# A decoder layer on one core: the split weights of each load at one of nine places in their buffers

## The chip, the core and the metric

The kernel runs on one core of a Trainium2 chip. The metric is the device time of one execution in microseconds (us). The profile is one execution of the program, recorded by the hardware profiler.

## The reference

One layer of a decoder (512 tokens, width 1024, float32): a SwiGLU feed-forward at half weight, a mixing block of three parallel head groups, a second SwiGLU feed-forward.

```python
def swiglu(x, w_gate, w_up, w_down):
    return (jax.nn.silu(x @ w_gate) * (x @ w_up)) @ w_down
...
x = x + 0.5 * swiglu(rms_norm(x, g_ffn1[l]), w_ffn1_gate[l], w_ffn1_up[l], w_ffn1_down[l])
h = rms_norm(x, g_mix[l])
proj = h @ w_in[l]
...
x = x + jnp.concatenate([y_attn, y_conv, y_mem], axis=-1) @ w_out[l]
x = x + 0.5 * swiglu(rms_norm(x, g_ffn2[l]), w_ffn2_gate[l], w_ffn2_up[l], w_ffn2_down[l])
```

The three groups are windowed attention with sinks, a causal depthwise convolution with LayerNorm, and cross-attention into 256 memory tokens. The feed-forward's inner width is 2816, that is 22 blocks of 128.

## The kernel before

Everything is kept transposed: channels on the 128 partitions, the 512 tokens along the free dimension. A float32 product is taken in three matmuls of type float32r. Each operand is split into a high half (rounded to float32r) and a low half (the rest), and `mm3` (line 339) and `product` (line 439) issue, for every block of 128x128 weights, high weights by high activations, high weights by low activations, low weights by high activations. Each of the three loads its weights anew. So TensorE's lists are long trains of triples: one weight load of 128 columns and one stream of 256 or 512 columns each.

The class `Weights` (line 86) brings the weights in. A load is 128 partitions by 1024 float32, by DMA from the SP queue into one of four raw buffers (`wraw`), up to three ahead. `split_to` (line 145) then splits it: ScalarE copies raw to the high half `hi` (line 167), VectorE writes raw minus hi to the low half `lo` (line 168). There are four pairs of buffers for halves, `whi0` to `whi3` and `wlo0` to `wlo3`, taken in turn (`self.turn`). Each has 1024 + 32 columns, so the 1024 that are used can begin anywhere in the first 128 bytes: `hi` begins at `off` bytes, `lo` at 128 - `off`. The caller gives `off` for each load: 0 for the gate and up weights of the first four blocks, the projections, the output weights and the memory values; 128 for the gate and up pairs that go through the sums, the down weights and the memory keys. A last kind of half load, `off=None`, goes to buffers of its own, `vhi` and `vlo`.

Where the buffers lie is read from the built program. Every `whi` buffer starts at a multiple of 256 bytes, every `wlo` buffer at 128 modulo 256. So with `off` 0 both halves begin at 0 modulo 256, with `off` 128 both begin at 128 modulo 256; the blocks within them follow at steps of 512 bytes. `vhi` and `vlo` lie at 128 modulo 256. The moving operands (`xh`, `xl`, `hh`, `hl`, `yh`, `yl`, `bh`, `bl`, `mh`, `ml`) all begin at 64 modulo 256.

The stages: in each feed-forward, blocks 0 to 3 are direct products of 512 columns (`xh`, `xl`). Blocks 4 to 21 go through `fast` (line 448), a scheme with seven products of half size, each of 256 columns with operands `bh` and `bl`, of which one takes `vhi` and `vlo`. The down products (`hh`, `hl`) come in six rounds, a part of the inner width each; those of the first round stream 512 columns, later ones 256 in two cuts. Between the two feed-forwards lies the mixing block, with 512-column products (`xh`, `xl`, then `yh`, `yl`) and the attention, the convolution and the norms in an order written out by hand. The memory keys and values (operands `mh`, `ml`, 256 columns) come at block 17 of the first feed-forward; for the values the weights are the moving operand and the memory the stationary one (lines 646 to 648).

The order on each engine is the order of the program text; a wait comes from buffers and data alone.

Of the kernel before, what the change touches and what calls it, by code (L numbers as in the profile page):

```python
# [85 lines left out]
class Weights:  # L86
# [58 lines left out]
    def split_to(self, n):  # L145
        nc = self.nc
        while self.done < min(n, len(self.items)):
            i = self.done
            need, cols, off, src = self.items[i]
            self.load_to(need + 1)  # L150
            if need in self.after:
                self.after.pop(need)()
            if off is None:
                hi, lo = (self.extra.tile([P, cols], F32R, tag=t, name=f"{t}{i}", bufs=1) for t in ("vhi", "vlo"))
            else:

                j = self.turn % self.bufs[1]
                self.turn += 1
                hi, lo = (
                    self.pool.tile([P, 1024 + 32], F32R, tag=f"{t}{j}", name=f"{t}{i}", bufs=1)[:, c : c + 1024]  # L160
                    for t, c in (("whi", off // 4), ("wlo", 32 - off // 4))
                )
            if i < self.by_hand:
                self.piece[i] = (src(), hi, lo)
            else:
                raw = src()
                nc.scalar.copy(hi[:, :cols], raw[:, :cols])  # L167
                nc.vector.tensor_tensor(lo[:, :cols], raw[:, :cols], hi[:, :cols].bitcast(F32), op=ALU.subtract)  # L168
            self.split[i] = (hi, lo)
            self.done += 1  # L170
            if i >= self.by_hand:
                self.load_to(need + 1 + self.dma_ahead)
# [1062 lines left out]
```

## Time and profile before

| | |
|---|---|
| time, two runs | 863.86 and 866.05 us, median 864.95 us |
| span of the profiled execution | 862.3 us |
| TensorE busy, weight loads busy | 855.5 us, 789.7 us |
| VectorE busy, ScalarE busy | 697.0 us, 446.1 us |
| TensorE clock granted | 1.00 |
| mean DMA rate | 106 GB/s |

The times are those of whole executions; the profiled execution is given by its span, the time from the first to the last instruction, which is 2.65 us below the median of the runs. PE stands for matmuls, PEld for weight loads, which overlap matmuls. Matmuls are pipelined, so the duration of one overlaps its neighbours. In groups, a row has the line, the engine, the operation, output and inputs by the program's names, shapes, count, busy time in us and mean in ns, and idle time before. In the timeline, a row has the start in us, the duration in us, engine, line, operation and names.

### The profile page before, as it was taken

What the parts mean: (1) busy time and instruction counts of PE and PEld (TensorE: products, weight loads), DVE (VectorE), ACT (ScalarE), POOL (GpSimd) and SP (SyncE); (2) the same over time, 40 slices, a digit from 0 to 9 for tenths busy, and PEclk for the clock granted to TensorE, in tenths of its full rate; (3) what the DMA queues carried; (4) which work ended last, traced back from release to release, by engine and by line L of the source; (5) the groups of instructions that cost most, each with busy time, mean ns of one, the idle gap of its engine ahead of it and who ended that gap; (6) DMA issues with size and microseconds to landing.
All of it is one profiled execution on the core that took longest, in us unless ns stands there. A gap on an engine that the chain in (4) does not pass through costs nothing.

```text
span 862.3 us, 15722 instructions
## 1 busy us (share of the span) xinstructions
PE 855.5 (99%) x6361; PEld 789.7 (92%) x6361; DVE 697.0 (81%) x1163; ACT 446.1 (52%) x741; POOL 27.4 (3%) x30
## 2 busy tenths in 40 slices
PE   9999999999999999999999999999999999999998
PEld 5889999999999999988776888889999999999998
DVE  7998877877868897869989985997887868787772
ACT  7455555455654444533948763454654544544540
POOL 0000000000000000300000030010000000000000
PEclk9999999999999999999999999999999999999999
DMA  7326333334553334222010423335333343323312
GB/s 273 123 78 168 97 100 122 100 112 133 142 143 120 123 110 130 74 98 62 5 57 14 133 75 103 94 91 154 99 98 123 98 122 97 109 92 100 120 49 99
DMA packets 34809, 91.45 MB, mean 106 GB/s; under 512 B 3248, under 2 KB 5808, under 8 KB 34736
## 3 DMA queue, kind: packets, MB, share of 16 engines
q1 hardware_dynamic: 32000, 85.99, 32.1%
q0 software_dynamic: 1584, 2.88, 2.1%
q10 hardware_dynamic: 1152, 1.57, 0.6%
q8 instruction: 50, 0.82, 0.4%
q14 instruction: 23, 0.19, 0.1%
HBM read 85.45 MB, written 2.10 MB: 102 GB/s over the span
## 4 chain that ended last, share of the span: by engine, by line
PE 92%; DVE 3%; ACT 2%; issue 1%; DMA 1%; SPq 0%; ACTq 0%; DVEq 0%
PE mm L347 14%; PE mm L349 14%; PE mm L348 14%; PE mm L444 11%; PE mm L445 11%; PE mm L446 11%; PE sc L444 2%; PE sc L445 2%; PE sc L446 2%; PE sc L349 1%; PE sc L347 1%; PE sc L348 1%; PE tp L948 1%; PE tp L962 1%; ACT p L913 1%
## 5 line engine op out<-in xcount | busy, mean ns | idle before, releaser
L444 PE MATMUL mm<-bh,whi 128*128 128x256 f32 x864 | 238.8, 276 | 0.2 <-ACT kept L459 0.2
L445 PE MATMUL mm<-bl,whi 128*128 128x256 f32 x864 | 238.5, 276 | 0.0
L446 PE MATMUL mm<-bh,wlo 128*128 128x256 f32 x864 | 238.5, 276 | 0.0
L348 PE MATMUL mm<-hl,whi 128*128 128x256 f32 (+1 forms) x640 | 183.9, 288 | 0.0
L349 PE MATMUL mm<-hh,wlo 128*128 128x256 f32 (+1 forms) x640 | 183.9, 288 | 0.0
L347 PE MATMUL mm<-hh,whi 128*128 128x256 f32 (+1 forms) x640 | 183.3, 288 | 0.0
L167 ACT CAST whi<-wraw 128x1024 fp32r<-128x1024 f32 (+2 forms) x122 | 124.2, 1021 | 102.5 <-PE mm L348 37.9
L168 DVE TENSOR_TENSOR wlo<-wraw,whi 128x1024 fp32r<-128x1024 f32 (+2 forms) x122 | 144.5, 1187 | 27.9 <-ACT whi L167 27.3
L444 PEld LDWEIGHTS mm<-bh,whi 128*128 128x128 f32 x864 | 162.2, 188 | 0.6 <-ACT kept L459 0.4
L445 PEld LDWEIGHTS mm<-bl,whi 128*128 128x128 f32 x864 | 162.2, 188 | 0.2
L446 PEld LDWEIGHTS mm<-bh,wlo 128*128 128x128 f32 x864 | 162.2, 188 | 0.0
L349 PEld LDWEIGHTS mm<-hh,wlo 128*128 128x128 f32 x640 | 120.2, 188 | 2.9
L347 PEld LDWEIGHTS mm<-hh,whi 128*128 128x128 f32 x640 | 120.2, 188 | 2.7
L348 PEld LDWEIGHTS mm<-hl,whi 128*128 128x128 f32 x640 | 120.2, 188 | 2.7
L168 DVE TENSOR_TENSOR wlo<-s,whi 128x1024 fp32r<-128x1024 f32 x72 | 87.9, 1222 | 34.7 <-ACT whi L167 34.4
L167 ACT CAST whi<-s 128x1024 fp32r<-128x1024 f32 x72 | 75.5, 1051 | 46.1 <-PE mm L445 42.3
L347 PE MATMUL mm<-xh,whi 128*128 128x512 f32 x192 | 76.6, 403 | 0.3 <-ACT whi L179 0.3
L348 PE MATMUL mm<-xl,whi 128*128 128x512 f32 x192 | 75.6, 394 | 0.6 <-DVE xl L359 0.5
L349 PE MATMUL mm<-xh,wlo 128*128 128x512 f32 x192 | 75.9, 395 | 0.0
L506 DVE SCALAR_TENSOR_TENSOR x<-mm,x 128x512 f32<-128x512 f32 x80 | 54.0, 682 | 3.3 <-PE mm L349 3.3
L167 ACT CAST vhi<-wraw 128x512 fp32r<-128x512 f32 x36 | 22.4, 622 | 60.9 <-PE sc L445 46.8
L126 DVE TENSOR_TENSOR s<-wraw 128x512 f32<-128x512 f32 x36 | 24.9, 691 | 33.5 <-DMA wraw<-in_wgu 33.5
(244 smaller groups left out, 1368.2 us busy)
## 6 DMA issues: line engine op xcount, KB each, us to landing
wraw<-in_wgu SPq DMA_DIRECT2D x86, 512.0 KB, 3.6
wraw<-in_wd SPq DMA_DIRECT2D x44, 512.0 KB, 3.6
wraw<-in_win SPq DMA_DIRECT2D x12, 512.0 KB, 3.5
x<-t POOLq DMA_DIRECT2D x8, 256.0 KB, 6.1
out<-t SPq DMA_DIRECT2D x7, 256.0 KB, 2.0
x<-in_xT SPq DMA_DIRECT2D x3, 512.0 KB, 6.8
wraw<-in_wout_a SPq DMA_DIRECT2D x6, 256.0 KB, 2.9
wraw<-in_wgu SPq DMA_DIRECT2D x4, 256.0 KB, 5.4
```

The costliest lines, as they stand in the source:

```text
L126: nc.vector.tensor_tensor(s12[:, l], u[:, l], u[:, r], op=ALU.add)
L167: nc.scalar.copy(hi[:, :cols], raw[:, :cols])
L168: nc.vector.tensor_tensor(lo[:, :cols], raw[:, :cols], hi[:, :cols].bitcast(F32), op=ALU.subtract)
L347: PE.matmul(ps[:, t], wh[:, w], hi(k)[:, t], start=one, stop=False, skip_group_check=cut > 1)
L348: PE.matmul(ps[:, t], wh[:, w], lo(k)[:, t], start=False, stop=False, skip_group_check=cut > 1)
L349: PE.matmul(ps[:, t], wl[:, w], hi(k)[:, t], start=False, stop=end, skip_group_check=cut > 1)
L444: PE.matmul(ps, wh[:, c], bh[k][:, block], start=one, stop=False, skip_group_check=not first)
L445: PE.matmul(ps, wh[:, c], bl[k][:, block], start=False, stop=False, skip_group_check=not first)
L446: PE.matmul(ps, wl[:, c], bh[k][:, block], start=False, stop=end, skip_group_check=not first)
L506: DVE.scalar_tensor_tensor(o, ps, 0.5, xd, op0=ALU.mult, op1=ALU.add)
L913: ACT.activation(self.p[n, h][:, c], src[h][:, i, c], AF.Exp, scale=self.fac[:, m : m + 1], bias=self.neg[:, m : m + 1], accum_out=self.de ...
L948: PE.transpose(ps[:, i * P : (i + 1) * P], self.p[n, h][:, c : c + P], ident)
```

## The change

`split_to` no longer places the two halves by `off`. It counts the splits, and the n-th split takes ph = n mod 9. The high half begins 16 x ph bytes into its buffer, the low half 16 x ((2 ph + 3) mod 9) bytes into its own. For ph = 0 to 8 the high half begins at 0, 16, 32, 48, 64, 80, 96, 112, 128 bytes, the low half at 48, 80, 112, 0, 32, 64, 96, 128, 16. Since the `wlo` buffers start at 128 modulo 256, the low halves lie at 176, 208, 240, 128, 160, 192, 224, 0 and 144 modulo 256. As there are four pairs of buffers and nine places, each buffer sees all places. `off` still tells `vhi` and `vlo` from the others, and for them nothing changes. The buffers' addresses, those of the moving operands of all products but the memory values, and the instructions and their order on every engine are as before.

```diff
             else:
 
                 j = self.turn % self.bufs[1]
+                ph = self.turn % 9
                 self.turn += 1
                 hi, lo = (
                     self.pool.tile([P, 1024 + 32], F32R, tag=f"{t}{j}", name=f"{t}{i}", bufs=1)[:, c : c + 1024]
-                    for t, c in (("whi", off // 4), ("wlo", 32 - off // 4))
+                    for t, c in (("whi", 4 * ph), ("wlo", 4 * ((2 * ph + 3) % 9)))
                 )
```

## The prediction

> **What bounds the kernel now.** I read the page's first and fourth parts, then the groups of TensorE kept apart by shape, then stretches of the timeline of TensorE.
>
> ```profile
> span 862.3 us, 15722 instructions
> PE 855.5 (99%) x6361; PEld 789.7 (92%) x6361; DVE 697.0 (81%) x1163; ACT 446.1 (52%) x741; POOL 27.4 (3%) x30
> PE 92%; DVE 3%; ACT 2%; issue 1%; DMA 1%; SPq 0%; ACTq 0%; DVEq 0%
> ```
>
> TensorE is busy in 99% of the span, and the chain of work that ended last lies on it for 92%. So the time is very nearly a count of matmuls times the interval at which they start. The count, by shape:
>
> ```profile
> L444 PE MATMUL mm<-bh,whi 128*128 128x256 f32 x864 | 238.8, 276 | 0.2 <-ACT kept L459 0.2
> L348 PE MATMUL mm<-hl,whi 128*128 128x256 f32 x576 | 159.0, 276 | 0.0
> L347 PE MATMUL mm<-xh,whi 128*128 128x512 f32 x192 | 76.6, 403 | 0.3 <-ACT whi L179 0.3
> L444 PE MATMUL sc<-bh,vhi 128*128 128x256 f32 x144 | 39.8, 276 | 0.0
> L347 PE MATMUL mm<-hh,whi 128*128 128x512 f32 x64 | 24.3, 395 | 0.0
> L347 PE MATMUL mm<-yh,whi 128*128 128x512 f32 x48 | 18.6, 405 | 1.1 <-DVE s L895 1.0
> L347 PE MATMUL sc<-xh,whi 128*128 128x512 f32 x32 | 12.6, 394 | 0.0
> L347 PE MATMUL sc<-yh,whi 128*128 128x512 f32 x16 | 6.1, 394 | 0.0
> ```
>
> Every such row stands for three matmuls, since a product is taken as high by high, high by low, low by high, each with its own weight load. In the buffers that the change touches there are 3 x (864 + 576) = 4320 matmuls of 256 columns and 3 x (192 + 48 + 32 + 16 + 64) = 1056 of 512 columns. The 3 x 144 with vhi and vlo lie in other buffers and stay as they are. The mean of one (276 or 395 ns) overlaps its neighbours, so it is not what one costs; the cost is the interval between starts, and that the timeline shows. First a stretch of 24 matmuls of 256 columns, from the first of a down product to the first of the next product:
>
> ```profile
> 699.94 0.28 PE L347 MATMUL mm<-hh,whi 128*128 128x256 f32 x1
> ...
> 702.66 0.28 PE L444 MATMUL mm<-bh,whi 128*128 128x256 f32 x1
> ```
>
> (702.66 - 699.94) / 24 = 113.3 ns. A stage of such matmuls alone keeps it up for 120 us, where TensorE has no idle time at all, while VectorE is idle for 30 and ScalarE for 62:
>
> ```profile
> 720.00:840.00 120.00, 120.00 (x1061) 120.00 (x1060) 89.76 (x116) 57.69 (x86) 0.00 (x0) 1.00 0.32 97
> ```
>
> Next, 72 matmuls of 512 columns in the first feed-forward's start (operands xh, xl), then 72 of the first round of its down products (hh, hl):
>
> ```profile
> 36.92 0.39 PE L349 MATMUL sc<-xh,wlo 128*128 128x512 f32 x1
> ...
> 53.40 0.40 PE L349 MATMUL mm<-xh,wlo 128*128 128x512 f32 x1
> 53.63 0.39 PE L347 MATMUL mm<-hh,whi 128*128 128x512 f32 x1
> ...
> 70.44 0.28 PE L444 MATMUL mm<-bh,whi 128*128 128x256 f32 x1
> ```
>
> (53.40 - 36.92) / 72 = 228.9 ns, and (70.44 - 53.63) / 72 = 233.5 ns. Both run on without a gap, both have 128x128 weights and 512 columns, and the granted clock is 1.00 throughout. What differs between them besides the data is where the weights lie: in the built program the moving operands start at 64 modulo 256 bytes in both, the weights at 0 modulo 256 in the first and at 128 in the second. That is 4.6 ns of 229, and the nearest thing in this trace to the price of a place. Last, the 48 matmuls of the memory keys, 256 columns, weights and moving operands at the very places modulo 256 that the 113.3 ns stretch has:
>
> ```profile
> 265.20 0.28 PE L348 MATMUL mm<-ml,whi 128*128 128x256 f32 x1
> ...
> 270.73 0.29 PE L646 MATMUL mm<-whi,mh 128*128 128x256 f32 x1
> ```
>
> (270.73 - 265.20) / 47 = 117.7 ns, right after a wait. So a train of the same form has two paces, 113.3 and 117.7, and holds one of them over dozens of matmuls. I read this as two reads of SBUF, the stream of one matmul and the weight load of the next, that fall into step or out of it.
>
> **The change part by part.** No instruction is added, removed or moved; each engine runs the same list in the same order with the same waits. Buffers, transfers and the number of buffers stay. Only addresses change, in three kinds of instruction.
>
> First, the splits write and read at other places, 16-byte steps instead of 0 or 128.
>
> ```profile
> L167 ACT CAST whi<-wraw 128x1024 fp32r<-128x1024 f32 x113 | 118.3, 1050 | 96.3 <-PE mm L348 31.8 <-issue 30.4 <-PE mm L445 22.6
> L167 ACT CAST whi<-s 128x1024 fp32r<-128x1024 f32 x72 | 75.5, 1051 | 46.1 <-PE mm L445 42.3 <-PE mm L647 2.0 <-PE mm L348 1.8
> L168 DVE TENSOR_TENSOR wlo<-wraw,whi 128x1024 fp32r<-128x1024 f32 x113 | 137.9, 1222 | 26.3 <-ACT whi L167 25.7
> L168 DVE TENSOR_TENSOR wlo<-s,whi 128x1024 fp32r<-128x1024 f32 x72 | 87.9, 1222 | 34.7 <-ACT whi L167 34.4
> ```
>
> The rows with s all have the 128-byte place and those with wraw mix it with 0: 1051 beside 1050 ns, 1222 beside 1222. I price this at nothing. The cover is large if I am wrong: 185 subtractions are 225.8 us, about a quarter of the span, and VectorE is idle for a quarter of the dense stage, so they would have to grow by most of their length before TensorE waited for them. At 10% longer they add 23 us to VectorE, all of it in its idle time.
>
> Second, the 4320 matmuls of 256 columns. Now the high half takes nine places and the low half nine others (its buffer starts at 128 modulo 256), so that weights start at each of the sixteen places modulo 256. No load keeps both halves at a place modulo 256 that it had. No row of this form has a weight off a multiple of 64 bytes. The bounds are from the nearest rows. Below, a train that is paced by weight loads with only 128 columns to stream: the transposes, as the chain of waits has them.
>
> ```profile
> 416.59 0.87 PE tp L948 x8
> 422.95 0.44 PE tp L1038 x4
> ```
>
> 0.87 / 8 = 108.8 ns each, that is 4.5 ns less than now. In the built program the weights of the first row (p) start 32 bytes past a multiple of 64, those of the second (t) at 128 modulo 256, and 0.44 / 4 = 110 is the same within the row's two digits: a load by itself does not mind its place, so it must be load and stream together that do. On the other side stand the 117.7 ns of the memory keys, 4.4 more, and, since nothing in the trace says that two paces are all there are, a second step of the same size (122 ns). I take the slower pace for two matmuls of three. The reason: in the sequence high, high, low the first two use one weight place, as now, and the passages from high to low and back now change it, which they do nowhere in the train at 113.3. So 2/3 x 4.4 = 2.9 ns on the mean, x 4320 = 12.7 us, all of it on the path, since TensorE has no idle time there to give.
>
> Third, the 1056 matmuls of 512 columns. The 864 that have weights at 0 run at 228.9 and go two thirds of the way to the other row: 2/3 x 4.6 = 3.1 ns, x 864 = 2.6 us. The 192 of the hh products stand on the slow row already and I leave them there; at the fast one they would give back 192 x 4.6 = 0.9 us.
>
> The Trainium skill speaks against any of this, in TensorE: Matmul & The Clock Gate, Part 2 (What happens when you issue a matmul), step 1: TensorE has two read ports, and "Loading the next tile's weights doesn't steal SBUF read bandwidth from the running matmul." By it the sum would be zero. The two stretches of 512 columns, 228.9 and 233.5, do not look like that, though they prove it only as far as their data are alike.
>
> Sum: 12.7 + 2.6 = 15.3 us, on the profiled execution's span 862.3, gives 877.6. The median of the runs shown, 864.95, is 2.65 above that span, so the time comes to 880.2, say **880 us**, 1.8% more. As a bound for one step everywhere: 4320 x 4.4 + 864 x 4.6 = 23.0 us, 888.
>
> **The rivals.** *Places do not matter.* The train at 113.3 is close to the 108.8 of weight loads with little to stream, so it may be the loads that set it, with room for a stall or two of the stream under them; and the 117.7 at equal places shows that something other than the place sets a pace. The 512-column rows speak against, but they are a fifth of the matmuls, and it takes the 256-column ones to move the time. Then 865, within 863 to 868. A rule of the Trainium skill leads the same way, SBUF — State Buffer, the note on cachelines under Door 1: lines are of 16 bytes and a crossing to a new one costs. Steps of 16 bytes leave the number of crossings alone, so by it too nothing changes; no run here shows a step that isn't a multiple of 16.
>
> *The new places are worse than any row.* Weights off a multiple of 64 bytes occur nowhere in the train, and six of the nine steps of each half are that. If beside a stream they cost a second step, the sum is 4320 x 8.8 + 864 x 9.2 + 192 x 4.6 = 46.8 us, 912; with one step everywhere it is 888, so this case holds 888 to 912. For it: the train has two paces and the two halves now go different ways in every load. Against: 4.4 to 4.6 ns is the only step seen, in both shapes, and the transposes show no price of a place 32 bytes off.
>
> *Faster: the passages between places break the collisions.* The 113.3 would be itself a pace with a collision in it, 4.5 ns over the 108.8 of the transposes, and weights that no longer stand in one relation to the stream would slip past it. At 108.8 throughout: 4320 x 4.5 = 19.4 us, 845.5. It decides from a mean of 109.3 ns (2% is 17.3 us, 4.0 ns each). For it only that the room exists; against it, that in the whole trace no stretch of this form runs under 113.
>
> **How the numbers follow.** My forecast, a slowing of one step for a part of the matmuls (870 to 890), 0.52; no effect 0.22; worse than the rows 0.20; faster 0.06. The likeliest value is 880. A measurement of this kernel tells about 2% from no change; that bound is at 882.2, and about four tenths of the forecast's own range lie above it (0.21). So slower by over 2%: 0.21 + 0.20 = 0.41; within 2%: 0.31 + 0.22 = 0.53; faster 0.06. The range 863 to 904 leaves out the faster case (0.06), the upper third of the worse case (0.07) and a little of the no-effect case.
>
> **What would show it.** The interval between starts, read off the timeline of TensorE load by load, should differ from load to load, with a mean near 116 in the 120 us stage (about 1033 matmuls instead of 1061 in the same stretch), 232 in the stretches of 512 columns, and unchanged 113 where vhi and vlo are used for whole triples. The splits should stay at 1050 and 1222 ns. If all loads still run at 113.3 and 229, the step that fails is that the place of the weights sets the pace; if some loads run far over 118 or well under 113, it is the size of the step. TensorE's waits for splits above today's would say that I misjudged the cover.

## The result and the profile after

The changed kernel takes **886.05 us** (two runs, 885.63 and 886.47) where the kernel before takes 864.95. The ratio is 1.0242, with an interval of 1.0209 to 1.0276. The profiled execution took 885.63 us with a span of 883.5 us. That is 21.2 us more span than before, and the medians of the runs differ by 21.1 us.

The page's first and fourth parts for the changed kernel (line numbers stand one higher than before, so 445 is the old 444):

```profile
span 883.5 us, 15722 instructions
PE 876.7 (99%) x6361; PEld 810.7 (92%) x6361; DVE 700.8 (79%) x1163; ACT 447.8 (51%) x741; POOL 27.5 (3%) x30
PE 96%; ACT 1%; DVE 1%; DMA 1%; issue 0%; SPq 0%; DVEq 0%
```

The same 6361 matmuls, and TensorE's busy time has grown by 876.7 - 855.5 = 21.2 us, exactly the growth of the span. Nothing was added to the chain by another engine. The groups by shape, for the matmuls and the splits:

```profile
L445 PE MATMUL mm<-bh,whi 128*128 128x256 f32 x864 | 242.1, 280 | 0.0
L349 PE MATMUL mm<-hl,whi 128*128 128x256 f32 x576 | 161.8, 281 | 0.0
L348 PE MATMUL mm<-xh,whi 128*128 128x512 f32 x192 | 76.7, 404 | 0.6 <-ACT xh L359 0.6
L168 ACT CAST whi<-wraw 128x1024 fp32r<-128x1024 f32 x113 | 118.1, 1048 | 108.9 <-PE mm L349 39.6 <-issue 32.2 <-PE mm L446 27.7
L169 DVE TENSOR_TENSOR wlo<-wraw,whi 128x1024 fp32r<-128x1024 f32 x113 | 138.2, 1224 | 38.5 <-ACT whi L168 38.0
L169 DVE TENSOR_TENSOR wlo<-s,whi 128x1024 fp32r<-128x1024 f32 x72 | 87.9, 1221 | 39.5 <-ACT whi L168 39.5
```

The splits cost what they did (1048 ns for 1050, 1224 and 1221 for 1222). The mean of a 256-column matmul rose from 276 to about 280 ns, but that mean overlaps its neighbours. The interval between starts shows the cost, here over 24 matmuls of the changed kernel's timeline of TensorE:

```profile
702.23 0.28 PE L445 MATMUL mm<-bh,whi 128*128 128x256 f32 x1
...
705.05 0.28 PE L445 MATMUL mm<-bh,whi 128*128 128x256 f32 x1
```

(705.05 - 702.23) / 24 = 117.5 ns, where such a stretch took 113.3 before. The view by stretches counts them over a longer time. Its columns are the stretch, its sum, then busy time with the number of instructions in brackets for matmuls, weight loads, VectorE, ScalarE and GpSimd, then the granted clock, the DMA share and GB/s. The first bracket is what matters here. The kernel before, from 31 to 53 us (512 columns) and from 630 us on (256 columns):

```profile
31.00:53.00 22.00, 22.00 (x98) 18.06 (x97) 21.89 (x33) 12.19 (x16) 0.00 (x0) 1.00 0.23 72
630.00:660.00 30.00, 30.00 (x267) 30.00 (x266) 24.60 (x34) 14.89 (x23) 0.00 (x0) 1.00 0.40 124
660.00:840.00 180.00, 180.00 (x1590) 180.00 (x1590) 136.80 (x176) 87.19 (x130) 0.00 (x0) 1.00 0.34 100
```

And the changed kernel, with the 120 us stretch that the prediction spoke of:

```profile
31.00:53.00 22.00, 22.00 (x97) 17.88 (x96) 21.73 (x32) 11.90 (x15) 0.00 (x0) 1.00 0.27 80
660.00:840.00 180.00, 180.00 (x1532) 180.00 (x1531) 135.01 (x173) 85.83 (x129) 0.00 (x0) 1.00 0.35 103
720.00:840.00 120.00, 120.00 (x1021) 120.00 (x1021) 88.34 (x114) 57.38 (x86) 0.00 (x0) 1.00 0.35 103
```

In 180 us TensorE starts 1532 matmuls instead of 1590, with no idle time in either and the clock at 1.00 in both. 180 us / 1590 = 113.2 ns, 180 us / 1532 = 117.5 ns.

From the start times of all matmuls in both traces the growth adds up. The means leave out the intervals around a wait; the growth is the sum of all intervals, waits included:

| matmuls | ns before | ns after | us of growth |
|---|---|---|---|
| 256 columns, whi and wlo (4320 and the memory keys) | 113.4 | 118.0 | 19.7 |
| 256 columns, vhi and vlo (432) | 113.4 | 114.8 | 0.6 |
| 512 columns, xh and xl (672) | 229.3 | 231.2 | 1.1 |
| 512 columns, yh and yl (192) | 229.4 | 231.7 | 0.3 |
| 512 columns, hh and hl (192) | 233.2 | 230.4 | -0.5 |

Together 21.2 us. Sorted by the places of the two halves modulo 256, the 256-column matmuls of the changed kernel are alike:

| high, low half at | 0, 176 | 16, 208 | 32, 240 | 48, 128 | 64, 160 | 80, 192 | 96, 224 | 112, 0 | 128, 144 |
|---|---|---|---|---|---|---|---|---|---|
| ns between starts | 117.8 | 117.9 | 117.4 | 117.3 | 118.9 | 119.2 | 118.1 | 118.0 | 117.8 |

No pair is near 113.3, not even the four that keep one half at 0 or 128.

### The profile page after: what moved, and what is told of

Same layout as the page of the kernel before. It is cut to its first block, busy times and chain, and to the rows that moved or that the text cites. A ratio compares the mean times of both kernels' runs of the same rounds, so it can differ in the third digit from the quotient of the medians.

```text
span 883.5 us, 15722 instructions
## 1 busy us (share of the span) xinstructions
PE 876.7 (99%) x6361; PEld 810.7 (92%) x6361; DVE 700.8 (79%) x1163; ACT 447.8 (51%) x741; POOL 27.5 (3%) x30
## 4 chain that ended last, share of the span: by engine, by line
PE 96%; ACT 1%; DVE 1%; DMA 1%; issue 0%; SPq 0%; DVEq 0%
PE mm L348 16%; PE mm L349 15%; PE mm L350 15%; PE mm L446 12%; PE mm L447 12%; PE mm L445 12%; PE sc L447 2%; PE sc L445 2%; PE sc L446 2%; PE sc L348 1%; PE sc L350 1%; PE sc L349 1%; PE tp L949 1%; PE tp L963 1%; ACT p L914 1%; DMA x<-in_xT 1%
## 5 line engine op out<-in xcount | busy, mean ns | idle before, releaser
L446 PE MATMUL mm<-bl,whi 128*128 128x256 f32 x864 | 242.7, 281 | 0.0
L447 PE MATMUL mm<-bh,wlo 128*128 128x256 f32 x864 | 242.4, 281 | 0.0
L445 PE MATMUL mm<-bh,whi 128*128 128x256 f32 x864 | 242.1, 280 | 0.0
L349 PE MATMUL mm<-hl,whi 128*128 128x256 f32 (+1 forms) x640 | 186.4, 292 | 0.0
L350 PE MATMUL mm<-hh,wlo 128*128 128x256 f32 (+1 forms) x640 | 186.0, 291 | 0.0
L348 PE MATMUL mm<-hh,whi 128*128 128x256 f32 (+1 forms) x640 | 185.5, 291 | 0.0
L169 DVE TENSOR_TENSOR wlo<-s,whi 128x1024 fp32r<-128x1024 f32 x72 | 87.9, 1221 | 39.5 <-ACT whi L168 39.5
L466 ACT ACTIVATE t<-t 128x512 f32<-128x512 f32 x36 | 22.8, 632 | 51.6 <-DVE t L465 51.4
```

Source lines behind the costliest of these rows:

```text
L348: PE.matmul(ps[:, t], wh[:, w], hi(k)[:, t], start=one, stop=False, skip_group_check=cut > 1)
L349: PE.matmul(ps[:, t], wh[:, w], lo(k)[:, t], start=False, stop=False, skip_group_check=cut > 1)
L350: PE.matmul(ps[:, t], wl[:, w], hi(k)[:, t], start=False, stop=end, skip_group_check=cut > 1)
L445: PE.matmul(ps, wh[:, c], bh[k][:, block], start=one, stop=False, skip_group_check=not first)
L446: PE.matmul(ps, wh[:, c], bl[k][:, block], start=False, stop=False, skip_group_check=not first)
L447: PE.matmul(ps, wl[:, c], bh[k][:, block], start=False, stop=end, skip_group_check=not first)
```

## The experiments

Every kernel below is the kernel before with the edit shown, so each is compared with that kernel, run on the same chip beside it. The text counts them in this order, from the first to the twelfth. All compute the same products; two of them add five small matmuls that nobody reads, as said there. In the expectations, A is the theory that each place has a price of its own; B, that it costs when the two halves lie at unequal places; C, that only weights off a multiple of 64 bytes cost; P, that only the passages between places cost, which was the prediction's reason. L, which the first four kernels suggested, is that the train has two paces and stays in the one it is in.

All rows of the view by stretches have the columns explained above.

**Both halves at one place, moving in 16-byte steps.**

```diff
+                ph = self.turn % 9
...
-                    self.pool.tile([P, 1024 + 32], F32R, tag=f"{t}{j}", name=f"{t}{i}", bufs=1)[:, c : c + 1024]
-                    for t, c in (("whi", off // 4), ("wlo", 32 - off // 4))
+                    self.pool.tile([P, 1024 + e], F32R, tag=f"{t}{j}", name=f"{t}{i}", bufs=1)[:, c : c + 1024]
+                    for t, e, c in (("whi", 32, 4 * ph), ("wlo", 64, 32 + 4 * ph))
```

> Both halves of a load lie at the same place modulo 256 bytes, and this common place goes through steps of 16 bytes from load to load, as in the changed kernel. Theory A (each place has its price; only 0 and 128 are good): most loads lie at new places, the 256-column matmuls run at about 118 ns in those, time 880 to 886 us. Theory B (the halves of one load at unequal places cost, since the weights' place then jumps inside each triple): the halves are equal, so 113.3 ns in nearly all loads, time 864 to 868 us. Theory C (only weights off a multiple of 64 bytes cost): 113.3 in loads at 0, 64, 128 and 192, 118 in the others, about 880 us.

Measured: 886.61 us, ratio 1.0227 (1.0135 to 1.0319). The kernel before, run beside this one and the next three, took 863.7 to 866.9 us in eight runs and 869.6 to 871.2 in seven, so the intervals of the four are wide. The stretch of 256 columns:

```profile
660.00:840.00 180.00, 180.00 (x1531) 180.00 (x1531) 133.97 (x171) 85.68 (x129) 0.00 (x0) 1.00 0.35 103
```

The halves are equal and the loss is all there, so it does not come from unequal halves: B falls, and with it the prediction's passages from high to low inside a triple. The mean of the whole train is 118.0 ns. The surprise is in the single loads: those with both halves at 128, the place that ran at 113.3 in the kernel before, took 117.8 ns here, all 16 of them. Those with both at 0 took from 113.5 to 117.8. So a price for each place does not explain it either. The loads at other places took 116.4 to 122.9 ns on the mean of a load.

**The two halves 128 bytes apart.**

```diff
-                    for t, c in (("whi", off // 4), ("wlo", 32 - off // 4))
+                    for t, c in (("whi", off // 4), ("wlo", off // 4))
```

> The high half stays where it is and the low half goes 128 bytes further: high at 128 and low at 0 modulo 256 in the pairs and down products, high at 0 and low at 128 in the direct loads. Both places are those of the kernel before, but unequal, and nothing changes from load to load. Theory A (places): 113.3 ns as before, 864 to 868 us. Theory B (unequal halves): 117 to 119 ns for the 4320 matmuls of 256 columns, 882 to 887 us. Theory C (off 64): 864 to 868 us. If the pattern repeats every 128 bytes, B expects no change here either.

Measured: 867.03 us, ratio 0.9988 (0.996 to 1.0016).

```profile
660.00:840.00 180.00, 180.00 (x1591) 180.00 (x1590) 137.01 (x177) 88.28 (x132) 0.00 (x0) 1.00 0.35 103
```

Here every triple has the passages from high to low and back, between 128 and 0, and 1591 matmuls run in the stretch as before. A passage of 128 bytes from one place to another is no cost in itself.

**The low half 16 bytes off, the same in every load.**

```diff
-                    for t, c in (("whi", off // 4), ("wlo", 32 - off // 4))
+                    for t, c in (("whi", 32), ("wlo", 4))
```

> Every high half at 128 modulo 256, every low half at 144, in all loads: one of the nine pairs of places of the changed kernel, without the change from load to load. Theory A or C (the low half alone is at a bad place, one weight load of three): a third of the step, 115 ns, 870 to 874 us. Theory B (unequal halves): the changed kernel's loads with this pair ran at 117.8, so 117.8 ns throughout, 883 to 888 us. If it is the change from load to load that costs, 113.3 ns and 865 to 870 us.

Measured: 883.58 us, ratio 1.0192 (1.0102 to 1.0283).

```profile
660.00:840.00 180.00, 180.00 (x1536) 180.00 (x1535) 136.32 (x175) 85.18 (x128) 0.00 (x0) 1.00 0.35 103
```

The high half lies at 128 in every load, as it did in this stretch before; only the low half has moved, to 144. One weight load in three is displaced, and all matmuls run at 117.75 ns. So no rotation over places is needed, and a third of the loads brings the whole step, not a third of it.

**The places 0 and 128 exchanged.**

```diff
-                    for t, c in (("whi", off // 4), ("wlo", 32 - off // 4))
+                    for t, c in (("whi", 32 - off // 4), ("wlo", off // 4))
```

> The two places of the kernel before are exchanged: the direct loads, projections and output weights (512 columns, operands xh and yh) at 128 modulo 256, the pairs and down weights at 0; both halves of a load equal. If the two rows of 512 columns (228.9 at 0, 233.5 at 128) differ by the place, xh and yh go to 233.5 (+4 us) and the first round of down products to 228.9 (-0.9 us); if they differ by the data, neither moves. For the 256 columns: theory B and C 113.3 ns as before, 865 to 869 us in all; theory A with 128 as the one good place for them 118 ns, 884 to 889 us.

Measured: 868.97 us, ratio 1.0012 (0.9985 to 1.004).

```profile
31.00:53.00 22.00, 22.00 (x96) 17.67 (x95) 21.51 (x31) 11.72 (x15) 0.00 (x0) 1.00 0.25 78
660.00:840.00 180.00, 180.00 (x1590) 180.00 (x1590) 137.40 (x178) 88.75 (x133) 0.00 (x0) 1.00 0.34 103
```

In the second stretch the 256-column train holds the fast pace at 0 as it did at 128. Five other stretches of this trace, of 7 to 22 us, ran at 117.8 at the same places. The 512-column products of the first stretch, now at 128, take 233.3 ns by their starts where they took 229.3 (xh) and 229.4 (yh). That the place decided there, which the prediction read from two stretches with other data, holds for them. The hh products, now at 0, do not follow fully: two of their eight loads run at 229 and six at 233.3. Nor is the place all there is to it for xh and yh: in the second kernel, where every load has one half at 0 and one at 128, some whole loads of theirs ran at 228.9 and others at 233.3.

**One load in nine displaced.** Its high half begins at 16 and its low half at 144 modulo 256, both 16 bytes off the old place modulo 128.

```diff
-                    for t, c in (("whi", off // 4), ("wlo", 32 - off // 4))
+                    for t, c in (("whi", 4 if self.turn % 9 == 5 else off // 4), ("wlo", 4 if self.turn % 9 == 5 else 32 - off // 4))
```

> The kernel before, with one load in nine at another place (high half at 16, low half at 144 modulo 256) and the other eight where they were. About 504 of the matmuls of 256 columns have displaced weights. Theory A (each load pays for its own place): these alone at 117.8, 504 x 4.4 ns = 2.2 us, 865 to 869 us. Theory L (the train has a fast and a slow pace, a displaced load throws it into the slow one, and it stays there until something releases it): loads at the old place that follow a displaced one also run at 117.8; with half to all of the train slow, 874 to 886 us.

Measured: 883.74 us, ratio 1.0209 (1.0178 to 1.0241). Nearly the whole loss, from a ninth of the loads. The timeline of TensorE around the first displaced load that feeds 256 columns, one row for every twelfth matmul:

```profile
73.38 0.28 PE L444 MATMUL mm<-bh,whi 128*128 128x256 f32 x1
...
74.73 0.28 PE L444 MATMUL mm<-bh,whi 128*128 128x256 f32 x1
...
76.10 0.28 PE L444 MATMUL mm<-bh,whi 128*128 128x256 f32 x1
...
77.51 0.28 PE L444 MATMUL sc<-bh,vhi 128*128 128x256 f32 x1
...
78.93 0.28 PE L444 MATMUL mm<-bh,whi 128*128 128x256 f32 x1
...
80.35 0.28 PE L444 MATMUL mm<-bh,whi 128*128 128x256 f32 x1
...
81.76 0.28 PE L444 MATMUL mm<-bh,whi 128*128 128x256 f32 x1
```

Steps of 1.35 and 1.37 us (113 ns each), and from the displaced load at 76.10 on steps of 1.41 or 1.42 (118 ns): in its own two products (from 76.10 and 78.93), in the vhi product between, which nothing displaced, and in the product at 80.35, whose weights are at 128 again. Over the whole run the matmuls whose two halves are at 128 average 117.5 ns, as theory L has it. They ran fast in one longer stretch, from 284 us, behind an interval of 202 ns, to the next displaced load at 314.6 us: 113.5 ns, and 117.9 from that load on.

**Every load at 16 and 144.**

```diff
-                    for t, c in (("whi", off // 4), ("wlo", 32 - off // 4))
+                    for t, c in (("whi", 4), ("wlo", 4))
```

> Every high half at 16, every low half at 144 modulo 256, in every load: places off a multiple of 64, but the same modulo 128 throughout, so that no passage from one load or half to the next changes the place modulo 128, but for vhi and vlo, which stay at 128. Theory A or C (the place itself): no load of 256 columns near 113.3, about 117, 880 to 886 us. Theory P (only passages cost, any common place is as good as another): 113.4 ns and 865 to 870 us.

Measured: 887.23 us, ratio 1.025 (1.0217 to 1.0282).

```profile
660.00:840.00 180.00, 180.00 (x1530) 180.00 (x1529) 133.54 (x171) 85.40 (x129) 0.00 (x0) 1.00 0.34 103
```

No load differs from the next, the halves are 128 apart as in the harmless second kernel, and each of the 144 loads that feed 256 columns runs at 117.8. The only passages left are those to vhi and back, so P falls but for them; the twelfth kernel takes them up.

**Every load at 64 and 192.**

```diff
-                    for t, c in (("whi", off // 4), ("wlo", 32 - off // 4))
+                    for t, c in (("whi", 16), ("wlo", 16))
```

> Every high half at 64, every low half at 192 modulo 256: a multiple of 64, the place modulo 128 of the moving operands themselves. The 64 bytes between weights and stream, which the kernel before has everywhere, are gone. If the distance to the stream is what lets the train run at 113.3: 118 to 120 ns, 882 to 892 us. If only alignment to 64 bytes is: 113.4 ns, 865 to 869 us. The 512 columns, at 228.2 in the few loads at this place so far, would give 1 us back.

Measured: 891.07 us, ratio 1.0294 (1.026 to 1.0328), the slowest of all.

```profile
660.00:840.00 180.00, 180.00 (x1518) 180.00 (x1517) 133.54 (x171) 84.89 (x127) 0.00 (x0) 1.00 0.34 103
```

The weights lie on a multiple of 64 bytes and run at 119.1 ns, so C falls. The moving operands also begin at 64, so weights and stream now stand at distance 0 modulo 128, where they stood at 64 in the kernel before and in the second and fourth kernels. The vhi products, left at 128, come back to 113.3 ns within about four matmuls in 32 of 36 cases; the other four stay at 117.7 to 117.9.

**The moving operands 32 bytes further, the weights where they were.**

```diff
-    tmp.tile([P, 32], F32, name="shift")
+    tmp.tile([P, 40], F32, name="shift")
```

> The weights stay where the kernel before has them, and all moving operands go 32 bytes up, to 96 modulo 256; vhi and vlo go along with them, to 160. If the place of the weights relative to the stream decides: the 4320 matmuls of 256 columns run near 117, the 432 with vhi and vlo, whose distance to the stream is unchanged, can keep 113.4; 878 to 886 us. If the weights' own place (their alignment) decides: 113.4 for the 4320, 865 to 869 us, and vhi and vlo, now off a multiple of 64, at 117.

This tile comes ahead of the moving operands, which go from 64 to 96 modulo 256; vhi and vlo move with them to 160. Measured: 888.57 us, ratio 1.0265 (1.0232 to 1.0298).

```profile
660.00:840.00 180.00, 180.00 (x1529) 180.00 (x1528) 133.42 (x171) 85.25 (x128) 0.00 (x0) 1.00 0.34 103
```

No weight of whi or wlo has moved, and the loss is all there (118.3 ns). And in the same timeline of TensorE, a down product of 24 matmuls, then a product with vhi and one with whi, 12 each:

```profile
664.99 0.28 PE L347 MATMUL mm<-hh,whi 128*128 128x256 f32 x1
...
667.82 0.28 PE L444 MATMUL sc<-bh,vhi 128*128 128x256 f32 x1
...
669.19 0.28 PE L444 MATMUL mm<-bh,whi 128*128 128x256 f32 x1
...
670.61 0.28 PE L347 MATMUL mm<-hh,whi 128*128 128x256 f32 x1
```

2.83 / 24 = 117.9, 1.37 / 12 = 114.2, 1.42 / 12 = 118.3. The middle one has weights at 160, off a multiple of 64, and a stream at 96: the distance is 64, and it is the fast one. The others have 128 and 96, the distance is 32. So it is not where the weights lie that allows the fast pace but how far they lie from the stream.

**One single load displaced.** Load 155 alone has its high half at 16 and its low half at 144 modulo 256; it serves two products of 12 matmuls in the second feed-forward.

```diff
-                    for t, c in (("whi", off // 4), ("wlo", 32 - off // 4))
+                    for t, c in (("whi", 4 if i == 155 else off // 4), ("wlo", 4 if i == 155 else 32 - off // 4))
```

> The kernel before with a single load displaced (item 155, 24 matmuls between about 621 and 624 us of the span; high half at 16, low half at 144 modulo 256). Theory A (a load pays for itself): 24 x 4.4 ns = 0.1 us, no change. Theory L (two paces, and the train stays in the one it is in): the train runs at 113.3 up to the displaced load and at 117.7 from there to the end, some 2070 matmuls x 4.4 ns = 9 us, 872 to 875 us.

Measured: 874.46 us (four runs), ratio 1.0099 (1.0083 to 1.0116), that is 8.7 us over the kernel before. By itself the load could cost 24 x 4.4 ns = 0.1 us. The timeline of TensorE, again every twelfth matmul:

```profile
621.97 0.28 PE L444 MATMUL mm<-bh,whi 128*128 128x256 f32 x1
...
623.34 0.28 PE L444 MATMUL mm<-bh,whi 128*128 128x256 f32 x1
...
624.75 0.28 PE L444 MATMUL mm<-bh,whi 128*128 128x256 f32 x1
...
626.16 0.28 PE L444 MATMUL mm<-bh,whi 128*128 128x256 f32 x1
```

From 623.34 to 626.16 the displaced load is in use, at 1.41 / 12 = 117.5 ns. From 626.16 on all weights are at 128 again, and the stretches behind it:

```profile
630.00:660.00 30.00, 30.00 (x257) 30.00 (x257) 24.08 (x34) 15.43 (x24) 0.00 (x0) 1.00 0.37 107
660.00:840.00 180.00, 180.00 (x1531) 180.00 (x1530) 133.67 (x170) 85.78 (x128) 0.00 (x0) 1.00 0.35 103
```

257 and 1531 where the kernel before has 267 and 1590, to the end of the dense work. 24 matmuls have pushed some two thousand behind them into the slow pace, and nothing in the train brings it back.

**The same load displaced, and a small matmul now and then.** Ahead of five of the second feed-forward's blocks a matmul of two columns is put into the train (its result is read by nobody); the first comes some 5 us behind the displaced load.

```diff
+            if last and f in (8, 11, 14, 17, 20):
+                PE.matmul(tp_bank()[:, 0:2], ident, pair, start=True, stop=True)
```

> The same single displaced load, and five small matmuls of two columns, whose output nobody reads, put in ahead of the blocks 8, 11, 14, 17 and 20 of the second feed-forward, at some 0.14 us each. Theory A: 0.7 us for the five, 866 us. Theory L: the slow pace holds between them, and a small matmul shifts weight loads against streams, so that at least one of the five ends it: 867 to 873 us, with the passages from one pace to the other at the displaced load and at the small matmuls and nowhere else.

Measured: 866.94 us (median of eight runs, 865.97 to 873.93, two of them over 871), ratio 1.0029 (1.0 to 1.0057). The timeline of TensorE around the first small matmul:

```profile
627.12 0.28 PE L444 MATMUL mm<-bh,whi 128*128 128x256 f32 x1
...
627.83 0.28 PE L444 MATMUL mm<-bh,whi 128*128 128x256 f32 x1
...
628.18 0.28 PE L454 MATMUL tp<-pair,ident 128*128 128x2 f32 x2
...
628.76 0.28 PE L444 MATMUL mm<-bh,whi 128*128 128x256 f32 x1
...
629.78 0.28 PE L444 MATMUL mm<-bh,whi 128*128 128x256 f32 x1
```

Ahead of it 0.71 / 6 = 118 ns, behind it 1.02 / 9 = 113.3. The same two stretches as for the ninth kernel:

```profile
630.00:660.00 30.00, 30.00 (x267) 30.00 (x266) 24.26 (x34) 15.28 (x24) 0.00 (x0) 1.00 0.44 124
660.00:840.00 180.00, 180.00 (x1590) 180.00 (x1589) 135.99 (x176) 87.74 (x131) 0.00 (x0) 1.00 0.34 100
```

267 and 1590, as in the kernel before. So the slow pace behind a displaced load is a state of the train that a disturbance can end, as L says. Here the small matmul made one interval of 204 ns; one of 118 followed, and from there on they were at 113. The two runs over 871 were not profiled.

**720 of the 512-column matmuls as two of 256 each.** Two at 113.3 would be 226.6 ns, under the 229 or 233 of one, so this would be a gain over the kernel before, if the pace held.

```diff
-                        True, True, woff=lo - j * (hi - lo), cut=1 + (r > 0 and not cut),
+                        True, True, woff=lo - j * (hi - lo), cut=1 + (not cut),
...
-                    mm3(g, gh, gl, range(8), xhk, xlk, True, True)
+                    mm3(g, gh, gl, range(8), xhk, xlk, True, True, cut=2)
...
-                    mm3(u, uh, ul, range(8), xhk, xlk, True, True)
+                    mm3(u, uh, ul, range(8), xhk, xlk, True, True, cut=2)
...
-        mm3(ps, wh, wl, range(8), xhk, xlk, True, True)
+        mm3(ps, wh, wl, range(8), xhk, xlk, True, True, cut=2)
```

> 720 of the 1056 matmuls of 512 columns taken as two of 256 columns (blocks 1 to 3 of gate and up, the first round of the down products, the projections); weights at the places of the kernel before. If such a pair runs at 2 x 113.3 = 226.7 ns instead of 229.3 (528 of them) and 233.3 (192): 1.4 + 1.3 = 2.7 us less, 862 us. If the passages between loads at 0 and at 128 throw the train into the slow pace, 2 x 117.7 = 235.4: 528 x 6.1 + 192 x 2.1 = 3.6 us more, and the slow pace carried into the trains behind it, up to 19 us more.

Measured: 883.74 us, ratio 1.0212 (1.0197 to 1.0228).

```profile
31.00:53.00 22.00, 22.00 (x190) 22.00 (x189) 22.00 (x33) 11.84 (x15) 0.00 (x0) 1.00 0.28 89
660.00:840.00 180.00, 180.00 (x1530) 180.00 (x1529) 135.97 (x174) 85.25 (x128) 0.00 (x0) 1.00 0.36 103
```

The gain did not come; the time went the way of the expectation's second case. Most of the new pairs ran at 117.8 (235.5 for a pair), at weights that lie 64 from the stream like all others: that distance allows the fast pace but does not bring it about. At 63 us the train passed to 113.3, behind an interval of 222 ns, and but for the memory keys it kept that to the end of the first feed-forward:

```profile
100.00:260.00 160.00, 160.00 (x1414) 160.00 (x1413) 126.79 (x168) 86.04 (x138) 2.58 (x3) 1.00 0.42 119
```

At 581 us, in the second feed-forward, an interval of 222 ns led the other way, from 113.3 to 117.8. The slow pace then held to the end, through the stretch from 660 to 840 us, in which no instruction was changed.

**Every load at 16 and 144, with the five small matmuls.** If the slow pace at 16 were only a state, a disturbance should end it there too.

```diff
-                    for t, c in (("whi", off // 4), ("wlo", 32 - off // 4))
+                    for t, c in (("whi", 4), ("wlo", 4))
...
+            if last and f in (8, 11, 14, 17, 20):
+                PE.matmul(tp_bank()[:, 0:2], ident, pair, start=True, stop=True)
```

> All high halves at 16, all low halves at 144 modulo 256, as in the run with that place throughout, and the five small matmuls of the run that ended the slow pace. If the slow pace there was only a matter of how the train was entered (a fast one exists at this place too): from the first small matmul on, at about 640 us, 113.3 ns, and some 7 to 9 us less than 887, that is 878 to 881 us. If this place has no fast pace: 117.8 ns on both sides of each, 887 to 889 us.

Measured: 887.83 us, ratio 1.0259 (1.0206 to 1.0313).

```profile
660.00:840.00 180.00, 180.00 (x1532) 180.00 (x1531) 133.40 (x171) 85.15 (x129) 0.00 (x0) 1.00 0.34 103
```

The small matmuls change the pattern of single intervals (from an even 117 to 119 to one such as 115, 117, 121, 117, 118, 123, 120, 113), and the mean of the run stays at 117.8. So does the mean of the 71 to 83 matmuls between each small matmul and the next vhi product, where no place changes. At this distance the train did not get fast, and P falls for the passages to vhi as well.

## Why the prediction was right, and where it was not

The forecast was 880 us with a range of 863 to 904; the time is 886.05, slower by 2.4%, on the upper side of the forecast's own range of 870 to 890. That it fell into that range is in part luck: the size of one step was read rightly, but the share of matmuls that pay it rested on a wrong reason. What the runs show of its steps:

**The splits at nothing: right.** 1048 ns for 1050 and 1224, 1221 for 1222; TensorE's longest wait stayed at 1.2 us and VectorE still was idle for a quarter of the dense stage. The cover was not needed.

**256 columns, "the slower pace for two matmuls of three": the step that failed.** It gave 2.9 ns on the mean and 12.7 us. The whole step was paid by nearly all of them: 4.6 ns on the mean, 19.7 us. The size of the step was read rightly, from the memory keys at 117.7. The reason for the two thirds was wrong: a passage of 128 bytes is free (unequal halves 128 apart, 0.9988), and the absence of passages does not help (equal halves, 1.0227; every load at 16 and 144, 1.025). Two facts stand in its place. The fast pace was held only where weights and stream begin 64 modulo 128 bytes apart; and a train that one displaced load has put into the slow pace stays in it after the weights are back in place, until something ends it. A third of the weight loads displaced gave 117.75 ns for all, a ninth of the loads 1.0209, one load 8.7 us. In the changed kernel every load has at least one half off that distance, so no load is left at 113.3. The prediction had the sign of this in hand, the memory keys that ran slow for 47 matmuls at good places, and took it as a price where it was a state.

**512 columns, 2/3 x 4.6 ns: a little too large, and the mechanism right in part.** 1.9 ns (xh) and 2.3 ns (yh) for 3.1, 1.4 us for 2.6. The hh products gave back 2.8 ns each, 0.5 us, where they were left at the slow row and 0.9 us was named as the most. Reading the two rows as prices of places was right in part: xh and yh went from 229.3 to 233.3 with the places exchanged, but hh at 0 showed both, and so did xh and yh with one half at 0 and one at 128. So 512 columns, too, have two paces at one and the same places.

**vhi and vlo unchanged: nearly.** 113.4 to 114.8 ns, 0.6 us. They lie where they lay, but come behind slow matmuls: 29 of their 36 products get back to 113.3 within four of their twelve matmuls, the other seven stay at 117.7 to 117.9.

**The bound, one step everywhere, 888: this is what happened,** less what hh gave back and xh and yh did not pay.

**What would show it.** Intervals that differ from load to load around 116 did not appear: the nine pairs lie between 117.3 and 119.2, and the 120 us stretch holds 1021 matmuls, not 1033. 231.2 and 231.7 for 512 columns came close to the 232 named.

**The rivals.** *Places do not matter* fell: with every instruction and wait alike, addresses alone moved the time by up to 2.9%. By what the prediction quoted from the Trainium skill, TensorE: Matmul & The Clock Gate, Part 2, that a weight load takes no read bandwidth from the running matmul, the sum would have been zero. The measured 113.3 against 117.8 to 119.1 ns from addresses alone does not agree with a sum of zero; whether it is read bandwidth that is lost, no run shows. What it drew from the Trainium skill, SBUF — State Buffer, the note on cachelines, that nothing changes, does not hold either: steps in multiples of 16 bytes, which keep the number of crossings, cost 1.9 to 2.9%. *Worse than any row*, a second step, did not come: no pair of places in the changed kernel is over 119.2 on the mean, and the worst fixed place that was tried, distance 0, has 119.1. *Faster* fell: in none of the traces read did a 256-column train hold a pace under 113.3.

**What stays open.** Why the distance between weights and stream matters, and modulo what exactly: that a stream and a weight load collide in reading SBUF would fit, and no run shows it. Distances of 0, 32 and 80 modulo 128 were held throughout and were slow; 16, 48, 96 and 112 occur only in loads between loads at other distances, as in the first kernel.

What puts a train at the good distance into one pace or the other is known only in part. In the traces of the kernel before and of the fourth, ninth, tenth and eleventh kernels such a train passed from 113 to 118 ns eleven times with nothing displaced, each time at an interval stretched to between 158 and 222 ns. One of them lies in the ninth kernel, 280 us ahead of its displaced load:

```profile
338.04 0.28 PE L347 MATMUL mm<-hh,whi 128*128 128x256 f32 x1
...
339.17 0.32 PE L348 MATMUL mm<-hl,whi 128*128 128x256 f32 x1
339.33 0.28 PE L349 MATMUL mm<-hh,wlo 128*128 128x256 f32 x1
...
343.69 0.28 PE L347 MATMUL mm<-hh,whi 128*128 128x256 f32 x1
```

(339.17 - 338.04) / 10 = 113 ns, then one interval of 160, then (343.69 - 339.33) / 37 = 117.8, and so on for 181 matmuls in all. The kernel before passes the same place with an interval of 154 ns and is back at 113 five intervals later. A stretched interval does not decide it alone: one of 204 ns ended the slow pace in the tenth kernel, and in the second kernel three passages came without one. The vhi products, too, go either way: all 36 got back to 113.3 in the third kernel, 32 in the seventh, but 3 in the fifth and 4 in the sixth. The kernel before itself took 870 us in some runs; slow stretches would make such a time, but none of those runs has a trace.

## What to carry to other kernels

Where TensorE is busy throughout, read the interval between starts of its matmuls, stretch by stretch, and not the duration of one: 113 against 118 ns hardly showed in the means (276 against 280), and was the whole of the 21 us. Keep stationary and moving operands at one distance in all loads of a train, and time a few distances, rather than spread the places; the good distance allows the fast pace but does not ensure it. Here one load of 24 matmuls at another place cost the train behind it 8.7 us.

## What was not expected of the hardware

- **The train keeps its pace.** After one displaced load of 24 matmuls the same code ran at 117.6 instead of 113.2 ns for over 200 us, and a matmul of two columns ended that (874.46 us without, 866.94 with five of them).
- **Distance, not place.** Moving the streams by 32 bytes and leaving the weights cost 2.65%, as much as moving the weights; vhi at 160 with the stream at 96 runs at 114.2 beside whi at 128 with the same stream at 118.3.
- **Displaced loads cost others more than themselves:** with one load in nine displaced, the undisplaced ran at 117.5, the displaced at 117.9.
